# The low parts of the recurrent gates' weights laid out on all 128 rows, in a two-layer hybrid block on one core

## The chip, the cores and the metric

The kernel runs on one core of one Trainium2 chip. The metric is the device time of one execution in microseconds, the median of several runs. Before the change it is 1859.09 us (three runs, 1857.01 to 1860.58).

## What is computed

Two layers of a transformer block over 512 tokens and 256 context tokens of 1024 features. A mixer of three branches (neighbourhood attention, latent attention, a gated linear recurrence) is followed by a feed-forward part, both modulated by adaLN. The change concerns the recurrence's gates, and in passing the rotary part of the latent keys. Cut to that:

```python
def _rglru_coeffs(xc, w_a, b_a, w_x, b_x, lam):
    xh = xf.reshape(B, L, LRU_HEADS, LRU_BLOCK)      # 4 heads of 64
    gate_a = jnp.einsum('blhi,dhij->dblhj', xh, w_a) + b_a
    gate_x = jnp.einsum('blhi,dhij->dblhj', xh, w_x) + b_x
    log_a = -LRU_C * jax.nn.sigmoid(gate_a) * jax.nn.softplus(-lam)
    a = jnp.exp(log_a)
    u = jnp.sqrt(-jnp.expm1(2.0 * log_a)) * (jax.nn.sigmoid(gate_x) * xf)
...
k_rope = _rmsnorm(kr, k_g[MLA_NOPE:])                # kr: 32 of the columns of u = x @ w_in
```

The index d is the direction of the scan (forward and backward); each of the four heads has its own 64 x 64 weights for the gates a and x.

## The kernel before

Features lie on the 128 rows, tokens (512 and then 256 of the context) on the columns. To keep float32 accuracy with the fast float32r format, every operand is split into a high part (a cast, `copy`) and a low part (the rest, `sub`), and a product is three passes: high by high, high by low, low by high. `split` (L576) does both; `lin` (L637) writes the passes down; `mm` (L497, the instruction is at L502) is one product, `tr` (L506, L507) a transpose on TensorE.

The gates are made in `lru_gates(f)` (L902), once for each tile f of two heads. The weights `st` [128 rows, direction x head x 128 columns] hold a head's 64 rows twice, once in each half of the rows. The operand `u[e]` of head e holds the high part of the head's 64 features in the head's own half of the rows ("mine") and the low part in the other half. So one product over 128 rows gives high by high and high by low at once, and the third pass, low weights by high operand, is a product over the head's own 64 rows alone:

```python
for o, k in segs(NT):                                                   # 512 columns, then 256
    mm(p[:, o : o + k], w[:, 0, c], u[e][:, o : o + k], True, False)
    mm(p[:, o : o + k], w[mine, 1, c], u[e][mine, o : o + k], False, True)
```

For each tile, two directions by two heads make four groups of four products into one PSUM tile each (`A`, two buffers, shared with the projections); two sigmoids on ScalarE (L927, L928) empty it. There are two tiles and two layers, so 16 groups.

`latent_rope` (L970) makes the shared rotary key. Its weights `w` have 64 columns of high and 64 of low parts side by side. By the operand's high part all 128 columns are multiplied (L984), by its low part only the 64 high ones (L983, L986).

The order of the program is not that of the text. `Order` records every operation with what it reads and writes and an assumed duration, and `place` (L304) then places all of them on the engines' clocks by a simple model, by rank and by earliest start; an operation that may run on several engines (a copy, a subtraction) gets its engine there. The steps of the mixer and their rank offsets are the table `PLAN` (L58). An added operation shifts the ranks behind it, and what an operation is assumed to take shifts the places. SyncE issues all loads in that order; `ast` (three buffers) takes the adaLN weights' rows, whose sums DVE and POOL make beside the other work (`ada_chunks`, L698) and TensorE adds up.

Of the kernel before, what the change touches and what calls it, by code (L numbers as in the profile page):

```python
# [13 lines left out]
ALU = mybir.AluOpType  # L14
# [6 lines left out]
KT = D // P  # L21
# [34 lines left out]
# The mixer's steps, each with its arguments, in the order in which they are written down, and after an @ how many  # L56
# operations a step ranks behind that place.
# [36 lines left out]
# ---------------------------------------------------------------------------------------------------------------  # L94
# Order of the program. The kernel is written down as a plain sequence of operations on buffers (Buf, views of them
# are Ref); Order works out what each depends on, places them on the engines' clocks by a simple model of what an
# operation takes, and then emits them in that order. Every wait is still Tile's.
# ---------------------------------------------------------------------------------------------------------------
# [30 lines left out]
class Ref:  # L129
# [50 lines left out]
    def spread(self, n):  # L180
        """[p, ...] -> [p, ..., n], the same element n times"""
        ix = np.broadcast_to(self.ix[..., None], self.ix.shape + (n,))
        return Ref(self.buf, self.chain + (("spread", n),), self.p, ix)
# [31 lines left out]
class ClockGate:  # L215
    """The tensor engine's clock: half after a window of little work, full after one of much."""
# [22 lines left out]
class Order:  # L239
    """engines: t (tensor), v (vector), s (scalar), g (gpsimd), d (loads and stores, issued by sync)"""  # L240
# [5 lines left out]
    def add(self, cost, emit, writes, reads, table=None, heat=1.0, middle=False):  # L246
        """cost: {engine: ns}; emit(engine); heat: how far a matrix product keeps the tensor engine's clock up; middle:
        neither the first nor the last product of a sum"""
# [7 lines left out]
        def meets(buf, e, p0, p1, m):  # L256
            q, a, b, k = e
            if not buf.psum:
                return k & m and a < p1 and p0 < b
            # one engine at a time on a tile, readers too; the tensor engine alone goes by banks  # L260
            return not (q.pe and op.pe) or (k & m and not (q.middle and middle))
# [42 lines left out]
    def place(self):  # L304
# [17 lines left out]
        while left:  # L322
            best = None
            for e, lst in avail.items():
# [36 lines left out]
                if len(top[1].cost) > 1:  # L361
                    # the engine that ends it first takes it
# [55 lines left out]
    def _weigh(self):  # L418
        """An operation's rank: where it stands in the program, and a little of how much hangs on it."""
# [38 lines left out]
def tile_block(ctx, tc, x_d, c_d, vec_d, con_d, mask_d, ada_d, ada0_d, win_d, wkr_d, wqk_d, wmv_d, gw_d, rpb_d, wout_d,  # L458
# [139 lines left out]
    def parts(n):  # L598
        """(stream, first column, columns): what the norms take one after the other"""
        return [(0, 0, NL), (1, NL, NC)] if n == NT else [(0, 0, NC), (0, NC, NC)]  # L600

# [35 lines left out]
    def lin(ps, pairs, n, rows=None, part=None):  # L637
        """ps[:, :n] = sum over ((whi, wlo), (xhi, xlo)) of w.T @ x, in three passes; of a part (first, size) of the
        columns alone, ps[:, :size]."""
# [7 lines left out]
    def rstd(sqs, groups, scale, n, rows=P):  # L647
        """1/sqrt(scale * sum of sqs over each group of rows + eps), in PSUM, on every row of its group:
        [(columns, tile)]"""
# [30 lines left out]
    def normed(ps, groups, scale, n, gains, rows=P, tag="tmp"):  # L680
        """rms-normalized rows of ps (over each group of rows) times gains [(columns, gain)], in SBUF"""
# [9 lines left out]
    def later(f, shift):  # L691
        """f's operations, after what is written down before and behind the next `shift` operations"""
# [5 lines left out]
    def ada_chunks(l, ch, nv):  # L698
        """mods[l] of the first nv streams, from the 4/nv times 256 columns of ada_w from ch*256: summed up by feature
        tile off the tensor engine, which then adds the partitions in four column groups at once."""  # L700
# [32 lines left out]
    def ada_cols(n, load, put):  # L733
        """n columns of the modulation on the tensor engine: the features of each of four row blocks add up in a column
        group of its own, and a product with the selector adds the four. load(kt): their weights' rows kt*128 and on;
        put(q): stores q [p, n/128, stream]."""
# [13 lines left out]
    def ada_later(c0):  # L750
        """mods[0] of 256 columns from c0"""
# [12 lines left out]
    def ada_first(c):  # L764
        """Scale (as a gain) and shift of the first mixer's feature tiles 2*c and 2*c + 1, on the tensor engine, which
        has nothing else to do yet."""
# [38 lines left out]
    def norm_mod(xs, h, r, k0, A, b, keep):  # L805
        """xs = h * A/rms + b of the feature tiles from k0, in two parts; r: 1/rms"""
# [10 lines left out]
    def weigh(src, p, nm, n, scale, total):  # L817
        """src [128 queries, n keys]: p = exp(scale * src + nm), total = its sum over the keys"""
        act(p[:, :n], src[:, :n], "Exp", bias=nm, scale=scale, accum=total)

    def p_transpose(p, nch, out):
        """p [128 q, nch*128 keys] -> out [128 keys, nch, 128 q]"""
# [11 lines left out]
    def scores(ps, o, q, k, order):  # L834
        """ps[:, o : o+n] = q.T @ k, the sum over the pairs of parts in order"""
# [7 lines left out]
    def values(o, view, pv, sums):  # L843
        """o = the two heads' values weighted by pv(e) = [(rows of values, weights, columns)], over the sums"""
# [14 lines left out]
    def mixer(l, xs, load_h, ready):  # L859
# [17 lines left out]
        # -- RG-LRU branch --  # L877
# [24 lines left out]
        def lru_gates(f):  # L902
# [4 lines left out]
            split(w[:, 0], w[:, 1], st)  # L907
            od.shift = 0
            # each head's operand: the high part in the head's half of the rows, the low part in the other
# [6 lines left out]
            for d in range(2):  # L916
                i = d * 2 + f
                sa[i], sx[i] = ta[:, d, :], tx[:, d, :]
                for e in range(2):
                    # a head's gates, the recurrence's in the head's half of the rows, the input's in the other  # L920
# [3 lines left out]
                    for o, k in segs(NT):  # L924
                        mm(p[:, o : o + k], w[:, 0, c], u[e][:, o : o + k], True, False)
                        mm(p[:, o : o + k], w[mine, 1, c], u[e][mine, o : o + k], False, True)
# [36 lines left out]
        # -- latent projections --  # L963
# [6 lines left out]
        def latent_rope():  # L970
# [6 lines left out]
            # rows 64 to 128 are the weights' low parts by the operand's high parts  # L977
            p = ps2()
            for k in range(KT):
                hi, lo = xs[k]  # L980
                for o, n in segs(NT):
                    if k:
                        mm(p[:64, o : o + n], w[:, k, :64], lo[:, o : o + n], False, False)  # L983
                    mm(p[:, o : o + n], w[:, k, :], hi[:, o : o + n], k == 0, k == KT - 1)  # L984
                    if not k:
                        mm(p[:64, o : o + n], w[:, k, :64], lo[:, o : o + n], False, False)  # L986
# [33 lines left out]
        # -- neighbourhood projections --  # L1020
# [11 lines left out]
        # -- latent attention --  # L1032
# [6 lines left out]
        # (query columns of 256, key segments, value chunks)  # L1039
# [80 lines left out]
        # -- neighbourhood attention --  # L1120
        near = {}

        def near_prep(m):
# [22 lines left out]
            # values of the four windows and of the context, keys on partitions  # L1146
# [18 lines left out]
        def na_bias(rpb, e):  # L1165
            mask = kept["mask"]
            """minus the bias, and 1e30 where the window ends"""
# [80 lines left out]
        # -- output projection and residual --  # L1248
# [10 lines left out]
    def deliver(l, h, fetch, xs, gate, n, normed_next):  # L1259
        """h += gate * (w.T @ xs), and the sums of squares for the norm that follows. The last tiles leave their second  # L1260
        part for while the first part's norm is on its way."""
# [39 lines left out]
    def decay(l):  # L1301
        """-8 and 8 times softplus(-lambda), per gate"""
# [53 lines left out]
    # the tensor engine's clock comes up with work, of which there is none before the first rows are here  # L1356
# [195 lines left out]
```

## Time and profile before

| what | value |
|---|---|
| median of three runs | 1859.09 us |
| lowest and highest | 1857.01 and 1860.58 us |
| profiled execution: span, first to last instruction | 1854.5 us |
| median minus that span | 4.6 us |
| TensorE busy | 1788.8 us, 96% |
| VectorE (DVE), GpSimd (POOL), ScalarE (ACT) busy | 59%, 39%, 26% |
| mean granted TensorE clock | 0.989 of full speed |

The page gives the profiled execution's span; a time of that execution with what lies around the span is not listed, and the difference to the median stands in its place. PE is the stream of products, PEld their weight loads, which run beside it. A row of a timeline merges equal neighbours: start, duration until the last one ends, engine, line, operation, tiles written and read, tile of TensorE as rows*columns, shape, count. A product's duration reaches past the start of the next, so pace is read from start to start.

### The profile page before, as it was taken

What the parts mean: (1) busy time and instruction counts of PE and PEld (TensorE: products, weight loads), DVE (VectorE), ACT (ScalarE), POOL (GpSimd) and SP (SyncE); (2) the same over time, 40 slices, a digit from 0 to 9 for tenths busy, and PEclk for the clock granted to TensorE, in tenths of its full rate; (3) what the DMA queues carried; (4) which work ended last, traced back from release to release, by engine and by line L of the source; (5) the groups of instructions that cost most, each with busy time, mean ns of one, the idle gap of its engine ahead of it and who ended that gap; (6) DMA issues with size and microseconds to landing.
All of it is one profiled execution on the core that took longest, in us unless ns stands there. A gap on an engine that the chain in (4) does not pass through costs nothing.

```text
span 1854.5 us, 25765 instructions
## 1 busy us (share of the span) xinstructions
PE 1788.8 (96%) x9880; PEld 1415.0 (76%) x9880; DVE 1100.5 (59%) x1847; ACT 481.0 (26%) x910; POOL 727.2 (39%) x691
## 2 busy tenths in 40 slices
PE   8999998899999999999999999999999999999999
PEld 4777765666778888888888887677677878888787
DVE  7666377897576556566634357676866544433443
ACT  4454264663030000000000013454564210000000
POOL 2433367777537766310121022245454222222222
PEclk9999999999999999999999999999999999999999
DMA  8111111323223343444422131121201222323233
GB/s 311 51 53 42 39 49 43 97 92 131 72 90 112 111 125 114 139 151 159 144 73 73 48 114 53 51 64 42 69 24 35 80 87 84 102 81 112 80 98 96
DMA packets 86380, 166.53 MB, mean 90 GB/s; under 512 B 9968, under 2 KB 51312, under 8 KB 86256
## 3 DMA queue, kind: packets, MB, share of 16 engines
q1 hardware_dynamic: 86256, 164.88, 27.8%
q8 instruction: 78, 1.28, 0.3%
q14 instruction: 46, 0.38, 0.1%
HBM read 160.65 MB, written 4.19 MB: 89 GB/s over the span
## 4 chain that ended last, share of the span: by engine, by line
PE 77%; DVE 10%; POOL 4%; DMA 3%; issue 3%; ACT 2%; SPq 0%; DVEq 0%; POOLq 0%; ACTq 0%
PE A L502 63%; PE B L502 10%; PE B L507 4%; DMA ast<-in_ada_dram 2%; DVE acc L570 2%; DVE s L537 1%; POOL rn L670 1%; DVE s L529 1%; POOL acc L537 1%; DVE tmp L529 1%; DVE tmp L537 1%; DVE sm L588 1%; ACT lo L516 1%; DVE wlo L537 1%; DMA hr<-in_x_dram 1%
## 5 line engine op out<-in xcount | busy, mean ns | idle before, releaser
L502 PE MATMUL A<-s,whi 128*128 128x512 f32 (+2 forms) x4340 | 1147.9, 356 | 8.1 <-ACT s L516 2.8
L502 PEld LDWEIGHTS A<-s,whi 128*128 128x128 f32 (+1 forms) x4340 | 760.9, 189 | 160.3 <-issue 16.2
L502 PE MATMUL A<-s,wlo 128*128 128x512 f32 (+1 forms) x2138 | 736.8, 355 | 1.9 <-POOL wlo L537 1.8
L502 PEld LDWEIGHTS A<-s,wlo 128*128 128x128 f32 x2138 | 397.5, 190 | 61.4 <-issue 7.6
L529 DVE CAST whi<-wst 128x1024 fp32r<-128x1024 f32 (+2 forms) x183 | 126.8, 693 | 408.1 <-PE A L502 356.5
L537 POOL TENSOR_TENSOR wlo<-wst,whi 128x640 fp32r<-128x640 f32 (+2 forms) x76 | 145.7, 1917 | 425.9 <-DVE whi L529 350.8
L570 DVE SCALAR_TENSOR_TENSOR acc<-ast,cc,acc 128x256 f32<-128x256 f32 x280 | 177.3, 633 | 103.4 <-DMA ast<-in_ada_dram 100.3
L516 ACT ACTIVATE tmp<-A 128x768 f32<-128x768 f32 (+1 forms) x75 | 55.2, 735 | 536.6 <-PE A L502 530.5
L537 DVE TENSOR_TENSOR wlo<-wst,whi 128x1024 fp32r<-128x1024 f32 (+3 forms) x132 | 165.6, 1255 | 7.3 <-POOL whi L531 2.1
L670 POOL TENSOR_TENSOR rn<-rn,con 128x12 f32<-128x12 f32 (+4 forms) x44 | 84.9, 1930 | 175.8 <-DVE rn L544 168.4
L502 PE MATMUL A<-s,s 128*128 128x512 f32 (+1 forms) x508 | 135.1, 366 | 15.1 <-ACT lo L516 9.0
L537 POOL TENSOR_TENSOR acc<-acc,ast 128x256 f32<-128x256 f32 x168 | 139.8, 832 | 9.9
L544 POOL TENSOR_SCALAR ast<-ast,cc 128x256 f32<-128x256 f32 x168 | 107.7, 643 | 75.9 <-DVE acc L570 71.3
L502 PEld LDWEIGHTS A<-s,s 128*128 128x128 f32 x508 | 82.0, 192 | 48.3 <-issue 19.4
L502 PE MATMUL B<-s,s 128*64 128x256 f32 (+2 forms) x720 | 110.5, 353 | 1.3 <-DVE s L529 1.3
L502 PE MATMUL B<-s,whi 128*128 128x512 f32 (+1 forms) x364 | 94.0, 346 | 2.4 <-DVE whi L529 1.8
L507 PE MATMUL B<-ident,tmp 128*128 128x128 f32 (+1 forms) x480 | 78.8, 278 | 15.3 <-ACT tmp L527 7.8
L507 PEld LDWEIGHTS B<-ident,tmp 128*128 128x128 f32 (+1 forms) x480 | 56.6, 142 | 38.5 <-ACT tmp L527 10.1
L531 POOL TENSOR_SCALAR whi<-wst 128x1024 fp32r<-128x1024 f32 (+4 forms) x23 | 28.9, 1259 | 141.1 <-PE A L502 91.1
L502 PEld LDWEIGHTS B<-s,s 128*64 128x64 f32 (+1 forms) x720 | 59.1, 144 | 28.5 <-issue 13.4
L531 POOL TENSOR_SCALAR s<-tmp 128x512 fp32r<-128x512 f32 (+2 forms) x24 | 29.9, 1245 | 125.8 <-DVE tmp L537 113.6
L527 ACT COPY s<-B 128x384 f32<-128x384 f32 (+2 forms) x149 | 67.7, 473 | 38.9 <-PE B L507 35.1
(169 smaller groups left out, 1752.7 us busy)
## 6 DMA issues: line engine op xcount, KB each, us to landing
ast<-in_ada_dram SPq DMA_DIRECT2D x320, 128.0 KB, 2.1
wst<-in_wg_dram SPq DMA_DIRECT2D x44, 512.0 KB, 3.5
wst<-in_wu_dram SPq DMA_DIRECT2D x44, 512.0 KB, 3.5
wst<-in_win_dram SPq DMA_DIRECT2D x32, 512.0 KB, 3.5
wst<-in_wd_dram SPq DMA_DIRECT2D x32, 384.0 KB, 3.1
wst<-in_wd_dram SPq DMA_DIRECT2D x32, 320.0 KB, 2.9
wst<-in_wout_dram SPq DMA_DIRECT2D x16, 512.0 KB, 3.4
hr<-in_x_dram SPq DMA_DIRECT2D x16, 384.0 KB, 4.1
```

What stands on the lines that cost most here:

```text
L502: od.add({"t": c / 2.4}, lambda e: nc.tensor.matmul(ap(out), lhsT=ap(lhsT), rhs=ap(rhs), start=start, stop=stop), [out], [lhsT, rhs], heat ...
L507: od.add({"t": 256 / 2.4}, lambda e: nc.tensor.transpose(ap(out), ap(in_), ap(ident)), [out], [in_, ident])
L516: nc.scalar.activation(ap(out), ap(in_), getattr(AF, func), scale=ap(scale), **kw)
L527: nc.scalar.copy(out=ap(out), in_=ap(in_))
L529: nc.vector.tensor_copy(ap(out), ap(in_))
L531: nc.gpsimd.tensor_scalar(out=ap(out), in0=ap(in_), scalar1=1.0, scalar2=1.0, op0=ALU.mult, op1=ALU.mult)
L537: (nc.vector if e == "v" else nc.gpsimd).tensor_tensor(out=ap(out), in0=ap(a), in1=ap(b), op=op)
L544: (nc.vector if e == "v" else nc.gpsimd).tensor_scalar(out=ap(out), in0=ap(a), scalar1=ap(s1), scalar2=ap(s2), op0=op0, **kw)
L570: lambda e: nc.vector.scalar_tensor_tensor(out=ap(out), in0=ap(a), scalar=ap(s), in1=ap(b), op0=op0, op1=op1),
L588: od.add({"v": 1.04 * in_.n + 65}, lambda e: nc.vector.reduce_max(ap(out), ap(in_), axis=AX.X, negate=True), [out], [in_])
L670: lambda e: nc.gpsimd.tensor_tensor(out=ap(r[:, :w]), in0=ap(r[:, :w]), in1=ap(C("mhalf", 0, w)), op=ALU.pow),
```

## The change

The low parts of a gate's weights, until now one subtraction over all 128 rows and 512 columns, are written by four subtractions, two for each head: the low part in the head's own half of the rows, and in the other half zero (the weights minus themselves). The second product then runs over all 128 rows: the other half, which holds the operand's low part, meets zeros. In `latent_rope` the operand's low part is multiplied by all 128 columns too, which adds low weights by low operand, and both operands' parts go through both column segments in turn. Docstrings and comments fall away; nothing else is edited.

```diff
@@ lru_gates (L902)
-            split(w[:, 0], w[:, 1], st)
+            copy(w[:, 0], st)
+
+            for e in range(2):
+                mine, other = halves(e)
+                of = lambda t: t.rearrange("p (d e c) -> p d e c", d=2, e=2)[:, :, e]
+                tt(of(w[mine, 1]), of(st[mine]), of(w[mine, 0].f32()), ALU.subtract)
+                tt(of(w[other, 1]), of(st[other]), of(st[other]), ALU.subtract)
             od.shift = 0
...
-                        mm(p[:, o : o + k], w[mine, 1, c], u[e][mine, o : o + k], False, True)
+                        mm(p[:, o : o + k], w[:, 1, c], u[e][:, o : o + k], False, True)
@@ latent_rope (L970)
             for k in range(KT):
-                hi, lo = xs[k]
-                for o, n in segs(NT):
-                    if k:
-                        mm(p[:64, o : o + n], w[:, k, :64], lo[:, o : o + n], False, False)
-                    mm(p[:, o : o + n], w[:, k, :], hi[:, o : o + n], k == 0, k == KT - 1)
-                    if not k:
-                        mm(p[:64, o : o + n], w[:, k, :64], lo[:, o : o + n], False, False)
+                for j, x in enumerate(xs[k]):
+                    for o, n in segs(NT):
+                        mm(p[:, o : o + n], w[:, k, :], x[:, o : o + n], k + j == 0, k + j == KT)
```

In layer 0 no other instruction changes its place. On POOL, the second weight split of layer 0 (`s` from `wst`) and the operand's low parts behind it (`s` from `lo`) stand like this before:

```order
L670 TENSOR_TENSOR rn_787<-rn_787,con_84 128x6
L531 TENSOR_SCALAR s_138_799<-wst_498 128x512
L531 TENSOR_SCALAR s_139_807<-lo_547 64x768
L537 TENSOR_TENSOR s_138_799<-wst_498,s_138_799 128x512
L531 TENSOR_SCALAR s_139_807<-lo_547 64x768
L537 TENSOR_TENSOR s_139_807<-lo_547,s_139_807 64x768 x2
```

and now:

```order
L670 TENSOR_TENSOR rn_790<-rn_790,con_84 128x6
L531 TENSOR_SCALAR s_138_802<-wst_514 128x512
L537 TENSOR_TENSOR s_138_802<-wst_514 64x2x128
L537 TENSOR_TENSOR s_138_802<-wst_514,s_138_802 64x2x128 x2
L537 TENSOR_TENSOR s_138_802<-wst_514 64x2x128
L531 TENSOR_SCALAR s_139_831<-lo_550 64x768 x2
L537 TENSOR_TENSOR s_139_831<-lo_550,s_139_831 64x768 x2
```

One subtraction became four, all ahead of the operand's two.

In layer 1 the places change too. On PE, around the third and fourth gate groups (`A` from `s` and `s`; `A` from `whi` and `wlo` is a key projection of another branch, `B` from `ident` the transposes of a row norm), before:

```order
L502 MATMUL B_10744<-s_1773_10280,whi_10725 128x512
L502 MATMUL A_10799<-s_1802_10537,whi_10575 128x512
L502 MATMUL A_10799<-s_1802_10537,whi_10575 128x256
L502 MATMUL A_10799<-s_1802_10537,whi_10575 128x512
L502 MATMUL A_10799<-s_1802_10537,whi_10575 128x256
L502 MATMUL A_10799<-s_1802_10537,wlo_10589 128x512
L502 MATMUL A_10799<-s_1802_10537,wlo_10589 128x256
L507 MATMUL B_10807<-ident_65,tmp_10794 128x128 x4
L507 MATMUL B_10749<-ident_65,tmp_10794 128x128 x2
L502 MATMUL A_10816<-s_1843_10705,s_1842_10505 128x512 x2
L502 MATMUL A_10816<-s_1843_10705,s_1842_10505 128x256 x2
```

and now:

```order
L502 MATMUL B_10753<-s_1773_10286,whi_10734 128x512
L502 MATMUL A_10810<-s_1843_10714,s_1842_10511 128x512 x2
L502 MATMUL A_10810<-s_1843_10714,s_1842_10511 128x256 x2
L507 MATMUL B_10816<-ident_65,tmp_10806 128x128 x4
L507 MATMUL B_10758<-ident_65,tmp_10806 128x128 x2
L502 MATMUL B_10753<-s_1773_10286,whi_10734 128x512
L502 MATMUL A_10826<-s_1843_10714,s_1842_10511 128x512 x2
L502 MATMUL A_10826<-s_1843_10714,s_1842_10511 128x256 x2
```

The third and fourth groups now stand ahead of the projection, which follows five products later.

On ACT, the copy that those transposes wait for (`tmp` from `rn`), which was DVE's, now stands between the sigmoids of the first two groups (`s` from `A`):

```order
L516 ACT_TABLE_LOAD
L516 ACTIVATE s_1844_10767<-A_10736,vec_7_126 64x768
L516 ACTIVATE s_1844_10767<-A_10762,vec_7_126 64x768
L516 ACTIVATE s_1845_10798<-A_10736,vec_7_126 64x768
L527 COPY tmp_10806<-rn_10775 128x768
L516 ACTIVATE s_1845_10798<-A_10762,vec_7_126 64x768
```

One more of these copies of the same layer moved from DVE to ACT, and behind the gates the casts and subtractions of the projections' weights are dealt anew between DVE, POOL and ACT.

## Rows read from the trace of the kernel before

**Rows 1.** The page, part 1: span, then busy time, share and instructions of each engine.

```profile
span 1854.5 us, 25765 instructions
PE 1788.8 (96%) x9880; PEld 1415.0 (76%) x9880; DVE 1100.5 (59%) x1847; ACT 481.0 (26%) x910; POOL 727.2 (39%) x691
```

**Rows 2.** The page, part 4: shares of the chain that ended last, by engine.

```profile
PE 77%; DVE 10%; POOL 4%; DMA 3%; issue 3%; ACT 2%; SPq 0%; DVEq 0%; POOLq 0%; ACTq 0%
```

**Rows 3.** Timeline of PE, one gate group: start, us, engine, line, operation, tile rows*columns.

```profile
95.82 1.44 PE L502 MATMUL A<-s,s 128*128 128x512 f32 x4
97.19 0.39 PE L507 MATMUL B<-ident,tmp 96*128 96x96 f32 x2
```

**Rows 4.** Timeline of PE's weight loads in the same group.

```profile
96.56 0.50 PEld L502 LDWEIGHTS A<-s,s 128*128 128x128 f32 x2 [0.25 <-issue]
```

**Rows 5.** Windows of layer 0, two gate groups: us, PE busy (pieces), PEclk, DMA, GB/s.

```profile
66.46:68.51 2.05, 2.05 (x4) 0.64 0.13 52
95.82:97.19 1.37, 1.37 (x6) 1.00 0.25 45
```

**Rows 6.** Chain that ended last, both mixers: start, us, what, how many.

```profile
78.36 0.97 DVE tmp L529
79.36 0.82 ACT tmp L516
111.79 8.07 PE A L502 x46
1199.90 1.73 PE A L502 x5
```

**Rows 7.** Layer 1: windows of two gate groups, and PE's timeline.

```profile
1175.87:1177.26 1.39, 1.39 (x6) 1.00 0.00 0
1194.13:1195.59 1.46, 1.46 (x8) 1.00 0.00 0
...
1185.40 0.87 PE L502 MATMUL A<-s,whi 128*128 128x512 f32 x4
```

**Rows 8.** Timeline and window of PE, layer 0, the shared rotary key's products.

```profile
54.46 6.34 PE L502 MATMUL A<-s,whi 128*128 128x512 f32 x35
54.46:60.63 6.17, 6.17 (x37) 1.00 0.24 85
```

**Rows 9.** Timeline of POOL in layer 0: after the first weight split, and the second.

```profile
16.61 0.72 POOL L537 TENSOR_TENSOR tmp<-tmp,tmp 128x256 f32<-128x256 f32 x1
50.80 0.10 POOL L582 MEMSET lam<- 128x4 f32 x1 [7.83 <-DVE lam L537]
87.98 1.29 POOL L537 TENSOR_TENSOR s<-wst,s 128x512 fp32r<-128x512 f32 x1
90.28 3.74 POOL L537 TENSOR_TENSOR s<-lo,s 64x768 fp32r<-64x768 f32 x2
```

**Rows 10.** Groups by form, POOL: busy us, mean ns | idle before.

```profile
L537 POOL TENSOR_TENSOR s<-hr,s 64x256 fp32r<-64x256 f32 x3 | 3.4, 1136 | 0.5 <-DVE s L529 0.3
```

**Rows 11.** Timelines of DVE and ACT in layer 1, between gate groups.

```profile
1182.83 0.68 DVE L537 TENSOR_TENSOR s<-wst,s 128x512 fp32r<-128x512 f32 x1
1181.52 3.64 ACT L516 ACTIVATE s<-A,vec 64x768 f32<-64x768 f32 x4
```

**Rows 12.** Waits of PE from 1200 to 1270 us: total, times, longest.

```profile
PE A L502 <- DVE s L537: 2.2, 2, 1.4
PE B L502 <- DVE whi L529: 1.8, 1, 1.8
```

**Rows 13.** Windows of layer 1 behind its gates.

```profile
1228.00:1246.00 18.00, 15.13 (x66) 0.91 0.23 76
1260.00:1266.00 6.00, 4.63 (x17) 0.72 0.00 0
```

**Rows 14.** Timeline of PE and chain, layer 0, where adaLN chunks run.

```profile
496.74 0.62 PE L502 MATMUL B<-acc,con 128*32 128x256 f32 x2 [1.68 <-DVE acc L570]
464.73 1.64 PE A L502 x9
```

## The prediction

> **What bounds the kernel now.** I read the page's busy times first, then the chain that ended last, and then the two stretches in which the gates are computed. TensorE is busy in 1788.8 of 1854.5 us [rows 1], and it holds 77% of the chain [rows 2]: what shortens its stream shortens the kernel, unless another engine is late at that place. The page gives the profiled execution's span alone, 1854.5 us; the median of the runs, 1859.1, lies 4.6 us above it, and I carry those 4.6 us over unchanged.
>
> The gates are 16 groups of four products, eight in each layer: for 512 columns and then for 256, one product over all 128 rows and one over 64. The reader is to see in one such group that TensorE has no idle mark and is nevertheless slow: the four products start at 95.82 and the next product starts at 97.19 [rows 3], so they take 1.37 us at full clock [rows 5]. A plain projection of the same mix (one product of 512 columns, one of 256) gives the pace to compare with: 46 products in 8.07 us are 0.175 us each [rows 6], so four should take 0.70. The surplus is **0.67 us a group**, and nobody is waited for: the weight loads of the group have gaps of 0.25 us put down to "issue" [rows 4]. Such a gap is what a product must show if its weights can't be loaded beside the product before it.
>
> Two groups of layer 1 take 1.39 and 1.46 us [rows 7]; the first of layer 0 ran at a mean granted clock of 0.64, between the levels of 1.2 and 2.4 GHz, and took 2.05 [rows 5]. All have the surplus, and what they have in common, and the projections have not, is the step from 128 rows to 64 and back.
>
> **The change part by part.**
>
> *Second pass over 128 rows.* 32 half-row products become 32 full ones with the same columns; nothing is added to TensorE's stream. By the pace above each group goes from 1.37 to 0.70, the first one from 2.05 to about 1.4 since its clock stays as it is: the wait ahead of it lies upstream. Bounds: at worst a group keeps a quarter of the surplus, 0.5 saved (the two products of a pair still share one PSUM range); at best all groups were of 1.46 and lose 0.76. I take 0.67, the undisturbed groups' value.
>
> How much lies on the path? In layer 0 the chain goes through every group but the third: there it leaves TensorE for a copy on DVE at 78.36 and one on ACT at 79.36 [rows 6], and the fourth group starts when they are done. So 7 x 0.67 = 4.7 us. In layer 1 all eight lie on a TensorE stretch of the chain, of which the piece at 1199.90 is one [rows 6], or beside one that waits for nothing else: 8 x 0.67 = 5.4 us. The sigmoids behind them, four in 3.64 us or 0.91 each [rows 11], two a group, need 1.8 us a group. Layer 1's eight groups lie between 1175.87 [rows 7] and beyond 1199.90 [rows 6], over 3 us apart on average, so ACT doesn't become the bound.
>
> *The split of the weights.* One subtraction over 128 x 512 becomes four over 64 rows by 256 elements. On POOL the old one took 1.29 us [rows 9]. For the new form the trace has 0.72 us for 256 elements on all rows [rows 9] and 1.14 for 64 x 256 under contention [rows 10], so four take 2.9 to 4.5 us: **1.6 to 3.3 us more**. In layer 0 the first split is covered, POOL is idle for 7.83 us before its next operation at 50.80 [rows 9]. The second is not: the operand's two products behind it end at 94.02 [rows 9], and the fifth group starts at 95.82 [rows 3], 1.8 us later. TensorE will be there 2.0 us earlier (groups one, two and four), POOL only 1.3 (its chain hangs on the third group's way through DVE and ACT). So 1.8 - 0.7 = 1.1 us of cover for 1.6 to 3.3 us: a stall of 0.5 to 2.2, or none if the group needs only the first of the two products. I take **0.5**, from the 0.72 row: it is nearest by its number of elements, and the 1.29 us of the old subtraction, 0.65 for 256 elements, lies beside it.
>
> In layer 1 the first split is again on an idle POOL and the second on DVE at 1182.83, 0.68 us now [rows 11]. Four at half of that or at the whole of it are 0.7 to 2.0 us more. It feeds only the last four groups, of which the first stands at 1194.13 [rows 7], 11 us behind. Cost nothing; if that cover went, at most 2.0.
>
> *The rotary key's products.* They keep their number and columns of data; 64 columns of weights become 128, so the small second order product is added. In the present program 35 products, 16 of 64 columns among them, run from 54.46 to 60.63 [rows 8], 0.176 us each: they stream at the full pace already. Cost and gain nothing; the cover is the product itself, beside which a 128-column load runs everywhere else. The Trainium skill, "TensorEngine Tiling (Array Packing)", sections Tiling Modes and Key Properties, counts half the rows and half the columns alike as tiling modes and says that changing the mode drains TensorE; by it both kinds of product pay, and the sum would be 10.6 us larger. For the rows the 0.67 us agrees; for the columns the 6.17 us disagree, and the measurement decides.
>
> *What moves.* Layer 0 keeps its order. In layer 1 the third and fourth gate groups go ahead of a projection, and two of the row norms' copies go from DVE to ACT. The third group then needs a PSUM tile that ACT frees with its third sigmoid; ACT begins at 1181.52 [rows 11], so 2.7 us later, 1184.3, less 0.7 gained: 1183.6. TensorE reaches that place, 1185.40 now [rows 7], 1.3 us earlier, 1184.1. No stall, but little room. Behind the gates TensorE waits for DVE's weight and operand splits, 2.2 and 1.8 us in the largest rows [rows 12], and runs at a lower mean clock, 0.91 over 18 us and 0.72 over 6 [rows 13], which is 1.6 and 1.7 us. The new order deals these waits anew. I see no reason for a sign, take nothing, and keep 4 us both ways for the range.
>
> Sum: 4.7 - 0.5 + 5.4 = **9.6 us**. Span 1854.5 - 9.6 = 1844.9; with the 4.6 around it **1849.5 us**, 0.5% faster.
>
> **The rivals.**
>
> *Layer 0's gain is eaten by the adaLN stream.* Between 430 and 500 us the chain runs through POOL, DVE and loads of adaLN rows, and TensorE waits 1.68 us for a sum at 496.74 [rows 14]. If that stream keeps its own pace, an earlier TensorE only waits longer, and 4.2 us are lost: 1859.1 - 5.4 = 1853.7. Against it: the chain enters that stretch from TensorE at 464.73 [rows 14], so the stream itself starts earlier. Chance 0.15.
>
> *The new order of layer 1 costs more than the gates give (slower).* Three row norms wait for their copy in ACT's queue there, two of them newly, and TensorE's transposes wait for that copy. Standing behind up to four sigmoids, 3.64 us [rows 11], three times, is 10.9 us; two more stretches of low clock like those of rows 13 are 3.3. That is 14.2 - 9.6 = 4.6 us slower, 1863.7. It decides from 13.3 us of new waits on. For it: the half microsecond of room above. Against: I find the copies due after the sigmoids ahead of them. Chance 0.06.
>
> *Nothing is saved.* The surplus would come from something other than the height of the tile, say from accumulating into the same PSUM range, and full tiles would cost the same: 1859.1, plus the 0.5 of POOL, 1859.6. Against it, the projections accumulate into one range too and stream at 0.175 [rows 6]. The Trainium skill, "TensorE: Matmul & The Clock Gate", Why this matters for your kernels, says that a small-K product takes the same time as a full one, which speaks against this change. Chance 0.05.
>
> *Column halves cost as row halves do.* Then the rotary key's products give back 0.33 us each as well, half of a group's 0.67: 32 x 0.33 = 10.6 more, 1838.9. Rows 8 speak against it. Chance 0.03.
>
> **How the numbers follow.** A measurement of this kernel can tell about 0.2%, 3.7 us, from no change. The forecast has the remaining 0.71. Its own range comes from the bounds: at best 16 x 0.76 = 12.2 and 4 from the waits, 1843; at worst 15 x 0.5 - 2.2 - 4 = 1.3, 1857.8. Both ends at once are unlikely, so I use 1843 to 1857: it takes in the adaLN rival and leaves out the other three, 0.14, and a little of the forecast's tail. Faster by over 0.2% (below 1855.4): 0.67 of the forecast, 0.11 of the adaLN rival, 0.03 of the columns, 0.81. Slower by over 0.2%: 0.06. The rest, 0.13, is no change.
>
> **What would show it.** Right: the gate groups of four take 0.70 to 0.8 us in both layers, the "issue" gaps between their weight loads are gone, and the rotary key's stretch still takes 6.2 us. POOL's second split in layer 0 takes 2.9 us or more and the fifth group waits for POOL by about half a microsecond. The stretch from the first gate to the first feed-forward product of each layer is 4 to 5 us shorter. Wrong: groups still at 1.37 (nothing saved); the wait at 496.74 longer by some 4 us (adaLN); transposes waiting for an ACT copy in layer 1 by several us, with new stretches of low clock (order).

## Result: 15.5 us faster, 0.8%, of which about 10 belong to the change

The changed kernel takes 1844.34 us (median of four runs, 1840.35 to 1846.99) beside 1859.84 us of the kernel before (four runs): a ratio of 0.9925, 95% interval 0.9900 to 0.9951. Two more comparisons, on other chips, gave 0.9947 (0.9934 to 0.9960) and 0.9943 (0.9927 to 0.9960), 10.1 and 11.1 us. Single executions of 2436 to 8087 us, a slow state that this program falls into now and then, are left out of every median here. The forecast was 1849.5 us in a range of 1843 to 1857, a gain of 9.6.

The page of the changed kernel's profiled execution, its span and TensorE's row [rows 1]; this execution took 1840.35 us in all, 2.05 more than its span:

```profile
span 1838.3 us, 25772 instructions
...
PE 1773.1 (96%) x9880; PEld 1411.0 (77%) x9880; DVE 1100.5 (60%) x1850; ACT 481.4 (26%) x912; POOL 725.2 (39%) x698
```

The product count is the same, and TensorE is busy for 15.7 us less: the time came out of the products' pace and, for up to 6 us of this pair of executions, out of the clock (below), not out of waits. Windows of the changed kernel over the fifth gate group of layer 0 and the third of layer 1 (us, then PE, PEld, DVE, ACT and POOL busy with pieces, PEclk, DMA, GB/s) [rows 5, 7]:

```profile
93.47:94.18 0.71, 0.71 (x7) 0.62 (x6) 0.71 (x1) 0.00 (x0) 0.09 (x1) 1.00 0.00 0
1176.57:1177.27 0.70, 0.70 (x6) 0.60 (x5) 0.70 (x1) 0.68 (x2) 0.70 (x1) 1.00 0.53 184
```

A group that took 1.37 to 1.46 us takes 0.70 where nothing disturbs it (the second of layer 1, for one, takes 0.80). Its weight loads, on the timeline of PEld, now read without a gap where two were put down to "issue" [rows 4]:

```profile
93.35 0.77 PEld L502 LDWEIGHTS A<-s,s 128*128 128x128 f32 x4
```

The waits of TensorE, changed kernel, from 60 to 130 us (layer 0's gates; total, times, longest). The first row stands ahead of the first gate and has its like before (2.08 us, for POOL). The others are new, but for 0.29 us for ACT that the kernel before had too:

```profile
PE B L502 <- ACT tmp L516: 1.7, 1, 1.7
PE B L507 <- DVE tmp L529: 1.5, 1, 1.5
PE A L502 <- ACT tmp L516: 0.7, 1, 0.7
PE A L502 <- ACT s L516: 0.6, 2, 0.3
```

The same view from 1170 to 1290 us, layer 1's gates and what follows:

```profile
PE B L507 <- ACT tmp L527: 3.3, 1, 3.3
PE A L502 <- DVE s L537: 2.1, 2, 1.3
PE A L502 <- ACT hr L527: 0.3, 1, 0.3
```

In the kernel before the waits of that view add up to 7.9 us (1.8 each for DVE's and POOL's weights, 2.2 for DVE's operands [rows 12], and four smaller ones); here they are 6.2, with the 0.3 and 0.2 that follow in the list.

At the adaLN sum that TensorE waited 1.68 us for [rows 14] the timeline of the changed kernel now has:

```profile
489.19 0.62 PE L502 MATMUL B<-acc,con 128*32 128x256 f32 x2 [0.26 <-DVE acc L570]
```

### The profile page after: what moved, and what is told of

Same layout as the page of the kernel before. It is cut to its first block, busy times and chain, and to the rows that moved or that the text cites. A ratio compares the mean times of both kernels' runs of the same rounds, so it can differ in the third digit from the quotient of the medians.

```text
span 1838.3 us, 25772 instructions
## 1 busy us (share of the span) xinstructions
PE 1773.1 (96%) x9880; PEld 1411.0 (77%) x9880; DVE 1100.5 (60%) x1850; ACT 481.4 (26%) x912; POOL 725.2 (39%) x698
## 4 chain that ended last, share of the span: by engine, by line
PE 77%; DVE 11%; POOL 3%; issue 3%; DMA 3%; ACT 2%; SPq 0%; DVEq 0%; POOLq 0%; ACTq 0%
PE A L502 62%; PE B L502 10%; PE B L507 4%; DMA ast<-in_ada_dram 2%; DVE acc L570 2%; DVE s L537 1%; POOL rn L670 1%; DVE s L529 1%; DVE wlo L537 1%; POOL acc L537 1%; ACT lo L516 1%; DVE lo L570 1%; DVE whi L529 1%; DVE lo L1300 1%; DVE tmp L537 1%
## 5 line engine op out<-in xcount | busy, mean ns | idle before, releaser
L502 PE MATMUL A<-s,whi 128*128 128x512 f32 (+1 forms) x4340 | 1144.8, 355 | 8.3 <-DVE s L537 2.7
L502 PEld LDWEIGHTS A<-s,whi 128*128 128x128 f32 x4340 | 759.8, 189 | 160.4 <-issue 16.6
L537 DVE TENSOR_TENSOR wlo<-wst,whi 128x1024 fp32r<-128x1024 f32 (+2 forms) x133 | 164.0, 1233 | 6.9 <-POOL whi L531 1.9
L502 PE MATMUL A<-s,s 128*128 128x512 f32 (+1 forms) x508 | 124.4, 353 | 13.8 <-ACT lo L516 9.2
L507 PE MATMUL B<-ident,tmp 128*128 128x128 f32 (+1 forms) x480 | 78.9, 278 | 19.5 <-ACT tmp L527 11.1
```

What stands on the lines that cost most here:

```text
L502: od.add({"t": c / 2.4}, lambda e: nc.tensor.matmul(ap(out), lhsT=ap(lhsT), rhs=ap(rhs), start=start, stop=stop), [out], [lhsT, rhs], heat ...
L507: od.add({"t": 256 / 2.4}, lambda e: nc.tensor.transpose(ap(out), ap(in_), ap(ident)), [out], [in_, ident])
L537: (nc.vector if e == "v" else nc.gpsimd).tensor_tensor(out=ap(out), in0=ap(a), in1=ap(b), op=op)
```

## Experiments

My theory: what is saved is the step from 128 rows to 64 and back, wherever it stands. Rivals: the new order did it; a half-row product is slow in itself; halves of columns cost the same. The diffs below are cut to what changes on the chip; where a run is said to be in a kernel's order, the planner was given that kernel's operations and costs.

**The changed kernel again, and the two halves of the change apart.** `after_again` is the changed kernel unedited.

> The changed kernel once more, beside the kernel before on the chip that the next three runs use. Every theory: 13 to 17 us faster than the kernel before, gate groups of 0.70 us. What is open is the clock: in the changed kernel's profiled run the records show 32 us of half clock, 42 in that of the kernel before. If the half-clock stretches go with the program and not with the run, the listed mean clocks of both kernels repeat themselves to 0.002, and the difference of about 5 us belongs to the change; if they fall by chance, the clocks of either kernel spread over both values.

Measured: 1847.71 us (six runs) beside 1857.85 of the kernel before (17 runs), 10.1 us faster, below the 13 to 17 that every theory expected; gate groups of 0.69 to 0.71 us where nothing disturbs them. The mean clocks of this kernel's runs spread over 0.988 to 0.991, those of the kernel before over 0.987 to 0.992: most of the spread goes with the run. A small part may go with the program: over all runs listed here the kernels with half-row products average 0.9889 (58 runs), the others 0.9897 (45, without one of 0.941), which is 1.5 us. The profiled execution of the first comparison, and that of this one (core, span, mean granted clock of TensorE):

```profile
core 0: 1838.3 us, clock 0.992
```

```profile
core 0: 1845.1 us, clock 0.988
```

The share below full speed is 0.008 x 1838.3 = 14.7 us in the one and 0.012 x 1845.1 = 22.1 in the other, 7.4 apart (the clock is rounded, so by about a microsecond either way), and their spans are 6.8 apart. The kernel before, at 0.989, lost 20.4 us so. By that, up to 6 of the first comparison's 16.2 us between the profiled executions are clock.

`half_new` is the changed kernel, in its order, with the second pass over the real rows:

```diff
-   mm(p[:, o : o + k], w[:, 1, c], u[e][:, o : o + k], False, True)
+   mm(p[:, o : o + k], w[mine, 1, c], u[e][mine, o : o + k], False, True)
```

> The changed kernel with its order, its weights' split and its rotary key's products, but with the second pass of the gates over the 64 real rows again. My theory, a product that steps from 128 rows to 64 and back costs 0.67 us per group of four wherever it stands: groups of 1.37 us, and 9 to 11 us slower than the changed kernel (16 groups by 0.67 are 10.7), or up to 16 if the half-clock stretches come back with them. Rival, the new order of layer 1 made the gain: groups of 1.37 but within 3 us of the changed kernel. Second rival, the groups were slow for their place beside other work and not for their rows: groups of 0.7 to 0.9 us here.

`full_old` is the kernel before, in its order, with the second pass over 128 rows, for which four subtractions stand in the place of the one:

```diff
-   mm(p[:, o : o + k], w[mine, 1, c], u[e][mine, o : o + k], False, True)
+   mm(p[:, o : o + k], w[:, 1, c], u[e][:, o : o + k], False, True)
```

> The kernel before with its own order and its own 64-column products of the rotary key, but with the second pass of the gates over 128 rows; the four small subtractions stand where the one stood. My theory: groups of 0.70 us, and 9 to 11 us faster than the kernel before; what the changed kernel has beyond that (15.5 in all, so some 5 us) is the new order's and the clock's. Rival, the order made the gain: within 3 us of the kernel before. If the half-clock stretches vanish with the row steps themselves, all 15 us are here already.

Measured, all on one chip:

| second pass | old order | new order |
|---|---|---|
| 64 rows | 1857.85 (kernel before) | 1857.51 (half_new) |
| 128 rows | 1847.53 (full_old) | 1847.71 (changed kernel) |

The rows are worth 10 us in either order, and the order nothing in either; both runs lie in the 9 to 11 us of my theory. The ratios to the kernel before are 0.9999 (0.9988 to 1.0010) for `half_new` and 0.9945 (0.9929 to 0.9960) for `full_old`. That rival has fallen, and with it any large part of the new waits: the 3.3 us for ACT's copy in layer 1 stand in `half_new` as well, and replace others.

`half_new` also shows what the prediction overlooked. Its timelines of PE and of the weight loads around the sixth group of layer 0:

```profile
101.16 1.45 PE L503 MATMUL A<-s,s 128*128 128x512 f32 x4
102.53 0.50 PE L503 MATMUL A<-s,whi 128*128 128x512 f32 x1
102.87 0.28 PE L503 MATMUL A<-s,wlo 128*128 128x256 f32 x1
```

```profile
101.48 0.18 PEld L503 LDWEIGHTS A<-s,s 64*128 64x128 f32 x1 [0.25 <-issue]
101.91 0.50 PEld L503 LDWEIGHTS A<-s,s 128*128 128x128 f32 x2 [0.24 <-issue]
```

The group takes 1.37, and the product of 512 columns behind it 0.34, start to start. In the changed kernel on the same chip the group takes 0.70 and that product 0.23 (timeline of PE, `after_again`):

```profile
95.07 0.86 PE L502 MATMUL A<-s,s 128*128 128x512 f32 x4
95.77 0.39 PE L502 MATMUL A<-s,whi 128*128 128x512 f32 x1
96.00 0.28 PE L502 MATMUL A<-s,wlo 128*128 128x256 f32 x1
```

So a group loses 0.67 + 0.11 = **0.78 us**, four steps of 0.195, and 16 groups 12.5 us. In layer 1 it can be read off: the first group starts 4.75 us later in `half_new` (1178.14 against 1173.39), and the transposes behind all eight groups 10.95 us later (at 1247.7 and 1236.7). That is 6.2 us, eight times 0.775.

**The rotary key's products.** `rope_half` is the changed kernel in its order, where the low operand meets 64 columns of weights again:

```diff
-   mm(p[:, o : o + n], w[:, k, :], lo[:, o : o + n], ...)
+   mm(p[:64, o : o + n], w[:, k, :64], lo[:, o : o + n], False, False)
```

> The changed kernel, where the second order product of the rotary key (low part of the weights by low part of the operand) is left out: the low operand meets 64 columns of weights again, in the kernel before's manner, in the changed kernel's order. My theory, half the columns cost nothing where half the rows do: within 1 us of the changed kernel, the rotary key's stretch of 35 products stays 6.2 us. Rival, a step in columns costs as much as a step in rows: 10 us slower, the stretch about 3 us longer.

Measured: 1846.97 us against 1847.71 of the changed kernel on the same chip. Timeline of PE, the 35 products and the next one:

```profile
54.13 6.35 PE L503 MATMUL A<-s,whi 128*128 128x512 f32 x35
60.32 0.40 PE L503 MATMUL A<-s,wlo 128*128 128x512 f32 x1
```

6.19 us, as with 128 columns (6.20 in `after_again`). Here half the columns cost nothing.

**Steps or half products?** `half_pairs` is `half_new` with each group sorted:

```diff
-   full 512, half 512, full 256, half 256
+   full 512, full 256, half 512, half 256
```

> The changed kernel with the second pass over the 64 real rows, but each gate group in another order: both full products (512, then 256 columns), then both half ones. A group then steps from 128 rows to 64 once and back once, where the kernel before did both twice. My theory, the step costs, not the half product: in the half-row form of this order a group's four starts lay 0.10, 0.20, 0.20 and 0.19 us over the pace, two of these steps go, groups of 1.0 us, and 5 us slower than the changed kernel. Rival, a half-row product is slow in itself, wherever it stands: groups of 1.37 us, 10 us slower.

`half_all` takes the first pass over 64 rows too:

```diff
-   mm(p[:, o : o + k], w[:, 0, c], u[e][:, o : o + k], True, False)
+   mm(p[:, o : o + k], w[mine, 0, c], u[e][mine, o : o + k], True, False)
```

> The changed kernel where both passes take 64 rows (left out: the high part of the weights by the low part of the operand). No step is left within a group, one into it and one out of it remain. My theory, the step costs: half products beside each other keep the pace, groups of 0.9 to 1.1 us as in the kernel with the products sorted. Rival, each half-row product costs 0.2 to 0.3 us more: groups of 1.4 to 2.0 us.

Measured: `half_pairs` 1851.06 us beside 1858.90 of the kernel before on its chip, ratio 0.9958 (0.9943 to 0.9973), so 7.8 us faster. The changed kernel did not run on that chip; by its ratios elsewhere (0.9943 and 0.9947) it would lie 2 to 3 us lower, where I had expected 5; the intervals are of that size. The kernel with the zeros by memset (below), which ran there, lies 6.2 lower; the totals don't settle the size, the starts in the trace do. `half_all` took 1852.31 us in its one run. Windows of `half_pairs` over a group and over the 512-column product behind it, and the weight loads:

```profile
98.98:99.96 0.98, 0.98 (x6) 0.49 (x4) 0.00 (x0) 0.00 (x0) 0.98 (x1) 1.00 0.09 17
99.96:100.30 0.34, 0.34 (x2) 0.30 (x2) 0.00 (x0) 0.23 (x1) 0.34 (x1) 1.00 0.00 0
```

```profile
98.87 0.31 PEld L503 LDWEIGHTS A<-s,s 128*128 128x128 f32 x2
99.42 0.29 PEld L503 LDWEIGHTS A<-s,s 64*128 64x128 f32 x2 [0.25 <-issue]
99.97 0.19 PEld L503 LDWEIGHTS A<-s,whi 128*128 128x128 f32 x1 [0.25 <-issue]
```

0.28 us over the pace in the group and 0.11 behind it: 0.39 us for two steps, 0.195 each again. Two gaps stand in the loads, one where the height falls and one where it rises; loads of one height follow each other without. The same windows and loads of `half_all`, where all four products have 64 rows:

```profile
102.09:102.98 0.89, 0.89 (x6) 0.66 (x5) 0.00 (x0) 0.00 (x0) 0.89 (x1) 1.00 0.00 0
102.98:103.32 0.34, 0.34 (x3) 0.30 (x3) 0.00 (x0) 0.24 (x1) 0.34 (x1) 1.00 0.00 0
```

```profile
102.08 0.76 PEld L503 LDWEIGHTS A<-s,s 64*128 64x128 f32 x4 [0.25 <-issue]
```

0.89 us, far from the 1.4 to 2.0 of the rival. From start to start the four take 0.34, 0.24, 0.12 and 0.20 us in the trace: inside the run of half products the second and third keep the full pace (0.23 for 512 columns, 0.12 for 256). What is left, 0.19 in the group and 0.11 behind it, with 0.09 ahead of it (the 256-column product before starts at 101.88 and the group at 102.09, where 0.12 is the pace), is 0.39 us for two steps again. The half product is not slow; the step is.

**Which heights?** `rows96` gives the second pass of one head 96 rows, 32 of them zeros:

```diff
-   mm(p[:, o : o + k], w[:, 1, c], u[e][:, o : o + k], False, True)
+   rows = slice(0, 96 if e == 0 else 128)
+   mm(p[:, o : o + k], w[rows, 1, c], u[e][rows, o : o + k], False, True)
```

> The changed kernel where the second pass of the first head takes rows 0 to 95 (its 64 real rows and 32 rows of zeros), that of the second head all 128. If any other number of rows costs a step, the first head's groups take 1.37 us like those of 64 rows and the time is 5 us longer. If only the step to a half costs, as the two 96-row transposes at 97.19 in the kernel before suggest, which with 0.17 us for the pair are no slower than 128-row ones, all groups stay at 0.70.

Measured: 1843.54 us in its one run, and such a group (window, and loads) shows neither a loss nor a gap:

```profile
94.23:94.94 0.71, 0.71 (x6) 0.62 (x5) 0.71 (x1) 0.00 (x0) 0.09 (x1) 1.00 0.00 0
```

```profile
94.12 0.78 PEld L503 LDWEIGHTS A<-s,s 128*128 128x128 f32 x4
```

A merged row prints the shape of its first member, so the 96-row loads are in it. By form (busy us, mean ns, idle before) they have 0.6 us of idle time before all 16 of them, none of it put down to "issue":

```profile
L503 PEld LDWEIGHTS A<-s,s 96*128 96x128 f32 x16 | 3.2, 198 | 0.6
```

Each product of the group keeps the pace, the 96-row ones too. So it isn't any change of height that costs: 64 does, 96 does not. Other heights weren't tried.

**What the split on POOL took back.** In the changed kernel POOL's second split, DVE's weight split and TensorE read like this (timelines of POOL, DVE and PE; start, us, what, idle before) [rows 9]:

```profile
84.66 0.80 POOL L537 TENSOR_TENSOR s<-wst 64x256 fp32r<-64x256 f32 x1
85.52 1.53 POOL L537 TENSOR_TENSOR s<-wst,s 64x256 fp32r<-64x256 f32 x2
87.11 0.61 POOL L537 TENSOR_TENSOR s<-wst 64x256 fp32r<-64x256 f32 x1
...
89.50 4.06 POOL L537 TENSOR_TENSOR s<-lo,s 64x768 fp32r<-64x768 f32 x2
```

```profile
89.92 1.96 DVE L529 CAST whi<-wst 128x1024 fp32r<-128x1024 f32 x1 [4.93 <-PE A L502]
91.98 2.67 DVE L537 TENSOR_TENSOR wlo<-wst,whi 128x1024 fp32r<-128x1024 f32 x1
...
99.82 0.56 DVE L529 COPY tmp<-rn 128x768 f32<-128x768 f32 x1 [2.46 <-POOL rn L670]
```

```profile
100.44 0.66 PE L507 MATMUL B<-ident,tmp 128*128 128x128 f32 x4 [1.46 <-DVE tmp L529]
```

The split takes 2.9 us where it took 1.29. The operand's subtractions behind it now lie over DVE's cast and subtraction, and that subtraction takes 2.67 us where it took 1.23 in the kernel before, with POOL done since 94.02:

```profile
94.67 1.23 DVE L537 TENSOR_TENSOR wlo<-wst,whi 128x1024 fp32r<-128x1024 f32 x1
```

The copy at the end of DVE's chain is late, and the transposes wait. It takes both, the longer split and the earlier TensorE, which starts DVE's cast: in `half_new` the split is as long, but DVE subtracts from 95.27, after POOL's end at 94.61, takes 1.23, and those transposes don't wait. `memset_same` is the changed kernel in its order, with the zeros by a memset:

```diff
-   tt(of(w[other, 1]), of(st[other]), of(st[other]), ALU.subtract)
+   memset(of(w[other, 1].f32()), 0.0)
```

> The changed kernel in its own order, where the zeros of the other head's half are written by a memset and not by subtracting the weights from themselves. In the changed kernel POOL's second split ends late, POOL's subtraction at 89.50 runs beside DVE's weight split, and the transposes at 100.44 wait 1.46 us for DVE. My theory, POOL's longer split does that: a memset of 64 x 256 takes under 0.6 us where the subtraction took 0.6 to 1.5, the wait shrinks below 0.7, and the kernel is 0.5 to 1.5 us faster than the changed one, less than five rounds can tell. Rival, the wait comes from the groups' being earlier alone: it stays 1.3 to 1.5 us, and nothing changes.

Measured: 1844.83 us beside 1858.90, ratio 0.9927 (0.9910 to 0.9944). The wait shrank to 1.09 only, DVE's subtraction still took 2.69 us, and another wait, at transposes ahead of it, grew to 1.0 from 0.3 (in `after_again`): my figure for the wait was missed, and no gain shows at that place.

The next three ran on one chip, to see whether the 4 us between this and the changed kernel's 10.1 were real.

> The changed kernel a third time, beside the next two on one chip. It was 15.5 us faster than the kernel before in the first comparison and 10.1 us in the second; the difference was put down to half-clock stretches that fall by chance. If so, 9 to 14 us here, with mean clocks that spread over 0.987 to 0.992 for both kernels.

> The kernel with the zeros by memset, in the changed kernel's order, once more: on another chip it was 14.1 us faster than the kernel before, where the changed kernel beside its own runs was 10.1 us faster. Its wait at the transposes shrank only to 1.09 us, and another grew from 0.3 to 1.0. My theory, the two are the same within 1.5 us and the 4 us lay in the clock and the chip. Rival, the shorter split is worth something that the profile does not show: 2 to 5 us faster than the changed kernel.

`sub_memset` keeps one subtraction for the low parts, as the kernel before, and clears the other head's halves behind it; the planner orders the program anew:

```diff
+   sub(w[:, 1], st, w[:, 0])
    for e in range(2):
-       tt(of(w[mine, 1]), of(st[mine]), of(w[mine, 0].f32()), ALU.subtract)
-       tt(of(w[other, 1]), of(st[other]), of(st[other]), ALU.subtract)
+       memset(of(w[other, 1].f32()), 0.0)
```

> A candidate: the low parts of all 128 rows by one subtraction, as in the kernel before, and then two memsets of the other head's half; the planner orders the program anew. POOL's split takes about 2.8 us where that of the changed kernel takes 3.6. I expect it within 3 us of the changed kernel, by the new order more than by the split; faster by over 3 us would make it the better version.

Measured beside 1856.38 us of the kernel before: the changed kernel 1845.23, so 11.1 us faster, in the 9 to 14 expected, `memset_again` 1847.41 (ratio 0.9942, 0.9924 to 0.9960), `sub_memset` 1843.75 (0.9931, 0.9915 to 0.9948). The memset alone is worth nothing that these runs can tell. The 4 us did not come back; whether they were chip, clock or chance isn't shown. In `sub_memset` POOL, DVE and PE read (timelines):

```profile
83.74 1.29 POOL L537 TENSOR_TENSOR s<-wst,s 128x512 fp32r<-128x512 f32 x1
...
85.89 0.65 POOL L582 MEMSET s<- 64x256 f32 x2
86.62 4.08 POOL L537 TENSOR_TENSOR s<-lo,s 64x768 fp32r<-64x768 f32 x2
```

```profile
88.02 0.99 DVE L529 CAST whi<-wst 128x1024 fp32r<-128x1024 f32 x1 [4.93 <-PE A L502]
89.11 2.68 DVE L537 TENSOR_TENSOR wlo<-wst,whi 128x1024 fp32r<-128x1024 f32 x1
```

```profile
97.59 0.66 PE L507 MATMUL B<-ident,tmp 128*128 128x128 f32 x4 [0.52 <-DVE tmp L529]
```

The split takes 1.9 us (1.29 and 0.65), DVE's cast 0.99 instead of 1.96, and the wait is 0.52 us. That is 0.9 us less than in the changed kernel, at the place where the split's price came out; since the order is new too, it supports that account and does not prove it. Split and wait go together: 2.9 and 1.46 us, 2.4 and 1.09 (`memset_same`), 1.9 and 0.52. What ties the two engines is in the rows. DVE's cast starts 0.42 us after POOL's pair in the changed kernel and 1.40 us after it in `sub_memset`, and ends 2.38 and 2.39 us after the pair's start; DVE's subtraction ends 1.09 us after the pair's end in both (94.65 and 93.56, 91.79 and 90.70). So POOL's place, which the split moves, and not DVE's own start times DVE's chain there. The medians differ by 1.5 us, within what these runs can tell: `sub_memset` is the shortest of the four kernels on that chip, but not shown to be faster than the changed one.

## Why the prediction was right, and where it wasn't

**The bound and the saving, right; the size of a group, too small.** The group's surplus was the step between 128 and 64 rows, nobody was waited for, and the undisturbed groups went from 1.37 to 0.70 us as forecast. The term that was mis-sized is the surplus: it was read from the group's first start to the next product's start, 0.67 us, and that product itself carries another 0.11. It measured 0.78, above even the best bound of 0.76. That 9.6 came so near to 10 is partly luck: 16 groups by 0.78 are 12.5, and the new waits in layer 0 took back about as much as each group had been sized too small.

**Layer 0, 4.7 minus 0.5 in the sum.** The undisturbed groups, the fifth to the eighth, gave 0.78 each; eight of them would be 6.2 us. Back went what the prediction had put into "the third group is off the chain": 0.26, 0.67 and 0.29 us for ACT at the third and fourth groups and behind them, 0.29 of which was there before. The stall of 0.5 us for POOL at the fifth group did not come; the group starts at 93.47 with no wait, just before POOL's pair ends at 93.56, so it needs only the first of the two. POOL's longer split, with TensorE earlier, cost 1.46 us in another place instead, through DVE, which the prediction did not look at because the instructions there were not edited. By these rows 6.2 - 0.9 - 1.5 = 3.8 us, where 4.2 was forecast; but that is a sum of rows. The stretch from the first group to the end of the eighth can be read directly in the kernel before and in `full_old`, which have one order (windows):

```profile
66.46:108.65 42.19, 41.85 (x194) 30.04 (x195) 19.74 (x41) 16.57 (x20) 14.61 (x12) 0.92 0.13 41
66.53:103.59 37.06, 34.06 (x194) 27.19 (x195) 20.67 (x41) 16.58 (x20) 16.40 (x15) 1.00 0.15 49
```

It is 5.1 us shorter. PE's busy time falls by 7.8, of which 0.08 x 42.19 = 3.4 is half clock that the kernel before alone had there, and its idle time grows from 0.3 to 3.0. At an equal clock the pace gave 4.4 us, near the 4.7 of the sum, and the waits took 2.7, where the sum had 0.5: 1.7 us are left of 4.2, and the waits are the term that was mis-sized. (A TensorE at half clock also hides waits, so the 1.7 may be too little.) All four profiled kernels with half-row products have half clock in this stretch (mean 0.84 to 0.92); of eight profiles of the others only two have (0.95). Whether the steps bring it on wasn't tried; the sum had no term for it.

**Layer 1, 5.4.** The groups gave 6.2 there, and the new order cost nothing, as taken: the waits there are 6.2 us where they were 7.9, dealt anew, and by the table above both orders take the same time. The rival of the new order has one row for it, the 3.3 us for ACT's copy. But that copy ran after ACT had waited 7.68 us for POOL, so it stood behind no sigmoid (timeline of ACT, changed kernel):

```profile
1231.23 0.62 ACT L527 COPY tmp<-rn 128x512 f32<-128x512 f32 x1 [7.68 <-POOL rn L670]
```

**The rotary key, nothing: right**, by 6.20 us and by `rope_half`. **The adaLN rival: wrong**, the wait shrank from 1.68 to 0.26 us. TensorE's waits for all such sums from 440 to 510 us add up to 2.8 us before, 0.3 in the changed kernel, 1.4 in `after_again` and 2.5 in `full_old`: they differ from run to run and are longer than before in none of these.

**Nothing is saved: wrong**, the rows are worth 10 us. The Trainium skill, "TensorE: Matmul & The Clock Gate", Why this matters for your kernels, says that a small-K product takes as long as a full one. That agrees with `half_all` inside a run of equal products (0.24 and 0.12 us). It leaves out the step, and the step is what the gain came from.

**Halves of columns: wrong here**, the 35 products take 6.19 us. The Trainium skill, "TensorEngine Tiling (Array Packing)", Key Properties, says that a change of tiling mode drains TensorE. The trace has a cost that fits this for 64 rows, 0.195 us a step, and none for these 64 columns.

**What lies around the span.** The 4.6 us were the median minus the span of an execution whose own time wasn't shown. In the changed kernel's profiled run it is 1840.35 - 1838.3 = 2.05, and about 2 in the other listed runs of it; so the other 2.6 were an execution faster than the median. With 2.0 the forecast would have been 1846.9, half of the way to the 1844.34 measured, and beside the 1847.71 and 1845.23 of the later comparisons. Most of what is left of the first comparison goes with the clock, for which the sum had no term.

## What to carry to other kernels

A product with 64 rows between full ones was no cheaper here and cost two steps of 0.2 us; fill the other half with zeros, or sort equal heights together. Look for it where TensorE never waits and yet runs under the pace of its plain products, with gaps in the weight loads put down to "issue"; and measure a surplus until the pace is regained, not until the next start. What the preparation of the zeros cost came out two engines further on, so time it at the wait that it feeds.

## What was not expected

96 rows cost no step, 64 do. And not all half columns are free as the rotary key's are. In the changed kernel's attention products of 64 columns stand between full ones; the loads of `after_again` show the gap where they end:

```profile
237.05 0.63 PEld L502 LDWEIGHTS B<-s,s 128*64 128x64 f32 x8
238.06 0.54 PEld L502 LDWEIGHTS A<-s,whi 128*128 128x128 f32 x3 [0.39 <-issue]
```

The first full product behind them, of 512 columns, starts at 238.07 and the next at 238.41: 0.34 us, the 0.11 over the pace that follows a step in rows. Three things set the two kinds of half columns apart in program and trace: the attention's write both halves of their output's rows in turn, in the trace they start in pairs (the second 0.01 us after the first, a pair every 0.21 to 0.27 us), and they are float32 products (`values`, L855), the rotary key's float32r. Which of these matters wasn't tried, and stays open. Nor is a late product alone the sign of a step: behind a transpose on the full tile (`after_again`, 100.70) the product of 512 columns, from 100.73 to 101.04, is late by 0.09 too, with no gap in the loads ahead of it. The steps of the gates show both, the gap and the late product.
